# One more pair of k tiles in block products, chunk 8's low part on VectorE, and a planner that knows GpSimd's queue

## The chip, the cores and the metric

The kernel runs on one core of a Trainium2 chip. The metric is device time in microseconds of one execution; lower is better. The five engines of the core that the profile names are TensorE (PE, with PEld for its weight loads), VectorE (DVE), ScalarE (ACT), GpSimd (POOL) and SyncE (SP, which here only requests transfers). Three executions are timed, and one is profiled.

## What is computed

A decoder trunk of two layers over 256 tokens of width 1024, in float32. Layer 0 mixes tokens by a chunked gMLP, layer 1 by block-sparse attention with a shared relative-position bias; each is followed by a gated MLP with a causal convolution of width 3, and each of the four sub-layers ends in a scaled residual and a LayerNorm. What the change touches is the second half of a layer:

```python
D_MODEL, SEQ, DEPTH, FFN_DIM = 1024, 256, 2, 2816
def conv_ffn(x, w_up, conv_w, conv_b, w_down):
    h = x @ w_up                                   # 256x1024 @ 1024x5632
    hp = jnp.pad(h, ((0, 0), (CONV_WIDTH - 1, 0), (0, 0)))
    hc = conv_b
    for j in range(CONV_WIDTH):
        hc = hc + conv_w[j] * hp[:, j:j + S]
    g, val = jnp.split(hc, 2, axis=-1)
    return (jax.nn.gelu(g) * val) @ w_down         # 256x2816 @ 2816x1024
# each sub-layer: x <- LayerNorm(alpha * x + f(x))
# attention adds bias_hb[:, rel_bucket(distance)] to its scores; the table has 32 buckets x 16 heads
```

## The kernel before, in words

**Products in three matmuls.** Every operand is held as two parts: a high part, rounded to the matmul's input type by ScalarE (`act`, L381), and a low part, the difference between the value and its rounding, by VectorE (`tt`, L387). A product is high by high, high by low and low by high, added up in PSUM. The weights of a down projection (2816 x 1024) come as 11 chunks of 1 MB; a chunk holds a pair of k tiles of 128 rows each, all 1024 columns, and goes as one load on SP's queue (`load`, L405) into one of two alternating buffers (`raw_75`, `raw_76`). `prep` then splits it into the tiles `whi` and `wlo`.

**Low parts by an adding transfer.** For the chunks that `ADDED` names, VectorE doesn't subtract: ScalarE writes the high part's negative into the low part's tile, and a transfer that GpSimd requests adds the chunk from memory to it (`lows`, L495). In `f_dn0` and `f_dn1` (the down projections of layers 0 and 1) these are chunks 1, 3 and 8.

**Seven block products.** A pair of k tiles against 256 tokens and 1024 columns is a product of 2 x 2 blocks by 2 x 2 blocks: 8 block products of 128 x 128 by 128 x 512, so 24 matmuls. For the pairs in `SEVEN` it is done by the scheme with seven products and sums of blocks on both sides: 21 matmuls. `weight_sums` makes the sums of weight blocks on VectorE and splits them, with ScalarE, into high and low parts; `token_sums` makes the sums of token blocks on GpSimd, four additions of 128 x 128 each in the tile `lnrow_80` (L634); `token_parts` splits those. `seven` issues the products, and after the last pair `into_rest` adds the common sums to the residual, before the last six k tiles (`TAIL`, chunks 8 to 10) finish the projection. The low parts of these pairs' plain blocks always come by an adding transfer of 0.5 MB (128 x 1024). `KINDS` says where a pair's split sums find room: beside the token parts (`early`, made before the projection starts), in `xt` (the transposed input, free by then), in `rr` (the first token tiles, when they have been used), or in `qk`. The raw rows of such a pair lie in the tile `raw_77`, or, for every other pair (`seven[1::2]`), in a part of the tile `ff`. In `f_dn1` the pairs are 5, 6 and 7.

**The order.** `Plan` records every operation with its engine, an assumed cost, the operations it depends on and a due time, then plays a list schedule for each engine and issues the instructions of an engine in the order of the starts that come out. TensorE's bulk matmuls keep the order in which they are recorded. On the chip an engine runs its instructions in that order and waits where an operand isn't there. Before, GpSimd's adding transfers are planned on an engine of their own, `gq`, beside `pool`, with the token sums; on the chip both are GpSimd's instructions.

**The bias table.** `build_bias` reads the table and a matrix that says which distance belongs to which bucket, rounds them into high and low parts on VectorE (L758, L760) and multiplies them in one matmul (L772), whose result VectorE copies (L774). This happens in the midst of layer 0's down projection. The roundings are recorded there as an operation of TensorE.

**The end of the last projection.** `with_sums` prepares for chunks 8 to 10 a copy of the last 256 columns, with the row sums beside them, in `xt` (ScalarE's operations of 128 x 256 and `xt<-stat` on VectorE), so that the last LayerNorm's mean comes out of the matmuls.

Of the kernel before, what the change touches and what calls it, by code (L numbers as in the profile page):

```python
# [25 lines left out]
NT = S // P  # L26
# [24 lines left out]
SOON = 5000.0  # L51
LEAD = 1700.0
WARM = 9
SEVEN = {"f_dn0": (4, 5, 6), "f_dn1": (5, 6, 7)}


KINDS = {"f_dn0": ('early', 'xt', 'rr'), "f_dn1": ('early', 'rr', 'qk')}


def part7(pairs, kinds):  # L60
# [6 lines left out]


PART7 = {name: part7(pairs, KINDS[name]) for name, pairs in SEVEN.items()}
ADDED = {"f_up0": {13: "act"}, "f_up1": {13: "act"}, "f_dn0": {1: "act", 3: "act", 8: "act"}, "f_dn1": {1: "act", 3: "act", 8: "act"}}  # L70
BESIDE = SEVEN


# [26 lines left out]
class Plan:  # L100
# [1 line left out]

    LATE = {"pe": 200.0, "act": 140.0, "dve": 130.0, "pool": 200.0, "sp": 910.0, "gq": 910.0}

    def __init__(self):
        self.ops, self.line, self.due = [], 0.0, []
# [36 lines left out]
    def emit(self):  # L145
# [24 lines left out]
        for o in ops:  # L170
            left[o] = len(o.deps)
            for d in o.deps:
                succ.setdefault(d, []).append(o)
        engines = ("pe", "act", "dve", "pool", "sp", "gq")
        free = dict.fromkeys(engines, 0.0)
        cand = {e: [] for e in engines}
        bus, table = 0.0, None
        order = []
        bulk = [o for o in ops if o.eng == "pe" and not o.fill]
        nb = 0  # L180
# [7 lines left out]
        while len(order) < len(ops):  # L188
            best = None
            for e in engines:  # L190
                c = cand[e]
                if e == "pe":
                    c = [x for x in c if x[1].fill or (nb < len(bulk) and x[1] is bulk[nb])]
                if not c:
                    continue
                s0 = min(max(free[e], r) for r, _ in c)
                now = [x for x in c if max(free[e], x[0]) <= s0 + 1.0]
                if e == "pe":
                    pick = min(now, key=lambda x: (not x[1].fill, x[1].due))
                else:  # L200
                    pick = min(now, key=lambda x: x[1].due)
                    for x in c:
                        s = max(free[e], x[0])
                        if x[1].due < pick[1].due and s0 < s < s0 + pick[1].ns and \
                                s + x[1].ns <= pick[1].due and x[1].due < s0 + pick[1].ns:
                            pick = x
                s = max(free[e], pick[0])
                if best is None or s < best[0]:
                    best = (s, e, pick)
            s, e, pick = best  # L210
            o = pick[1]
            cand[e].remove(pick)
            if o.eng == "pe" and not o.fill:
                nb += 1
            o.start = s
            if e == "gq":
                bus = max(bus, s + 1100.0) + o.nbytes / 360.0
                free[e] = s + 1200.0
                o.end = max(bus + 1000.0, s + 2000.0 + o.nbytes / 200.0)
            elif e == "sp":  # L220
                bus = max(bus, s + 1100.0) + o.nbytes / 360.0
                free[e] = max(s + 475.0, bus - 1500.0)
                o.end = bus
            else:
                extra = 0.0
                if o.table and o.table != table:
                    extra, table = 1300.0, o.table
                o.end = free[e] = s + o.ns + extra
            order.append(o)
            for x in succ.get(o, ()):  # L230
                left[x] -= 1
                if not left[x]:
                    cand[x.eng].append((ready(x), x))
# [16 lines left out]
        assert not held  # L250

    def lag(self, d, o):
        if d.eng == o.eng:
            return 0.0 if d.eng == "pe" else 910.0 if d.eng in ("sp", "gq") else 130.0
        return self.LATE[d.eng] + (150.0 if o.eng == "pe" else 0.0)


def flat(ap):
    n = 1
    for d in ap.shape[1:]:  # L260
        n *= d
    return n
# [3 lines left out]
def trunk_kernel(ctx: ExitStack, tc: tile.TileContext, a: dict, out: bass.AP):  # L266
# [221 lines left out]
    def lows(i, lv, hv, at, hs, ls, by):  # L488

        name, c = stream[i]  # L490
        if by == "act":
            act(lv, hv.bitcast(F32), AF.Copy, hs, ls, scale=-1.0)
        else:
            dve(70 + 0.52 * flat(lv), lambda: nc.vector.tensor_scalar_mul(lv, hv.bitcast(F32), -1.0), hs, ls)
        plan.op("gq", 3600 + 1.8 * flat(lv), lambda: nc.gpsimd.dma_start(  # L495
            lv, a[name][c][:, at:at + flat(lv)], accum_op=ALU.add, max_dma_last_dim=4 * SUB), (), ls, nbytes=flat(lv) * P * 4)

    def with_sums(key, hi, lo, raw, at):
# [247 lines left out]
    def build_bias(at):  # L746
# [15 lines left out]
        def clear():  # L762
# [5 lines left out]
        plan.op("sp", 4096 / 360, lambda: fill_in(a["rel_bias"], BUCKETS, slice(0, HEADS)), (), [raw], nbytes=4096)  # L768
        plan.op("sp", 65536 / 360, lambda: fill_in(a["onehot"], nb, slice(HEADS, n)), (), [raw], nbytes=65536)
        b = half()  # L770
        plan.op("pe", 645, parts, [raw], [b], True)
        state["table"] = plan.op("pe", 1, lambda: nc.tensor.matmul(  # L772
            b.ap[:HEADS, :DIST], cast[:two, :HEADS], cast[:two, HEADS:], start=True, stop=True), [raw], [b], True)
        dve(400, lambda: nc.vector.tensor_copy(row.ap[:HEADS], b.ap[:HEADS, :DIST]), [b], [row])  # L774
        scr = dram.tile([HEADS, DIST], F32, name="rbscr")
        s = Buf(scr)
        state["bias"] = load(scr, row.ap[:HEADS], [s], [row], nbytes=32768)
# [174 lines left out]
    def project_out(name, nk, at, xold, li, rows_i):  # L952
# [41 lines left out]
        for k, t in sorted(early, key=lambda x: x[1]) if nk == KT else early:  # L994
# [3 lines left out]
            elif k % 2 and t == NT - 1:  # L998
# [7 lines left out]
                if n == len(pairs7) - 1:  # L1006
                    into_rest(xold, extra)
                    by_x = 1.0
            if name == "f_dn0" and (k, t) == (3, NT - 1):
                state["table"].after = groups[-1]  # L1010
            if pairs7 and t == NT - 1:
                for n in range(len(pairs7)):
# [496 lines left out]
```

## Time and profile before

| | |
|---|---|
| time, median of 3 runs | 559.65 us (557.83 to 560.56) |
| profiled execution, its own time | 558.85 us |
| span of the profiled execution | 557.1 us |
| granted TensorE clock | 0.996 |
| PE, busy | 548.8 us (99%), 3024 matmuls |
| DVE, busy | 479.1 us (86%) |
| ACT, busy | 396.5 us (71%) |
| POOL, busy | 51.7 us (9%) |
| moved by the DMA engines | 122.51 MB |

In the profile's views a row of the timeline gives start, length, engine, line of the program, operation, what it writes and reads, and how many instructions it groups; in brackets the idle time of the engine ahead of it, and what ended it. Tiles are named without buffer numbers there: `raw` is any of `raw_75` to `raw_77`, `wlo` any of `wlo_70` to `wlo_74`, `lnrow` the tile of the token sums. The matmuls of a busy TensorE overlap; the step from one start to the next is their price. The last down projection starts at 492.1 us, its first seven block products at 519.3, and its last matmul ends at 550.4.

### The profile page before, as it was taken

The page shows a single profiled execution, that of the slowest core. Times are in us where ns is not written, and L with a number is a line of the kernel's source. Part 1 is how long each engine was busy: PE and PEld are TensorE (multiplying, and loading weights), DVE is VectorE, ACT ScalarE, POOL GpSimd, SP SyncE. Part 2 cuts the span into 40 slices and gives each one's busy share as a digit, 9 for nine tenths or more (in the row PEclk, how much of TensorE's full clock was granted, in tenths as well). Part 3 has the DMA queues.
Part 4 walks back from the last instruction along what each step waited for, and adds up shares of the span by engine and source line. Part 5 has one row for each costly group of instructions (what it writes and reads, how often), then busy time and mean ns, then how long its engine had stood idle before and what let it go on. Part 6 is the DMA issues. An engine that isn't in the chain of part 4 may idle for free.

```text
span 557.1 us, 8253 instructions
## 1 busy us (share of the span) xinstructions
PE 548.8 (99%) x3024; PEld 471.0 (85%) x3024; DVE 479.1 (86%) x860; ACT 396.5 (71%) x669; POOL 51.7 (9%) x60
## 2 busy tenths in 40 slices
PE   9999999999999999999999999999999999999995
PEld 6889888988898887888888888788888888888884
DVE  6699989999989888898957778798969889997687
ACT  6647576688878786845567868577747969897951
POOL 0011110000003521001000000000000000053101
PEclk9999999999999999999999999999999999999998
DMA  8979624645954799893656252725754956799832
GB/s 325 390 284 355 222 99 161 260 184 228 240 213 166 232 283 301 219 356 115 235 218 194 103 191 86 296 77 191 263 188 191 259 203 235 282 268 321 185 100 77
DMA packets 22610, 122.51 MB, mean 220 GB/s; under 512 B 2519, under 2 KB 5801, under 8 KB 10409
## 3 DMA queue, kind: packets, MB, share of 16 engines
q1 hardware_dynamic: 19240, 110.18, 53.4%
q0 software_dynamic: 3040, 11.54, 11.3%
q8 instruction: 24, 0.39, 0.3%
q10 hardware_dynamic: 288, 0.26, 0.1%
q14 instruction: 18, 0.14, 0.1%
HBM read 120.90 MB, written 1.07 MB: 219 GB/s over the span
## 4 chain that ended last, share of the span: by engine, by line
PE 63%; DVE 14%; DMA 12%; ACT 7%; issue 3%; DVEq 0%; SPq 0%; ACTq 0%
PE bank L369 40%; PE twos L369 22%; DVE wlo L387 5%; DMA raw<-in_f_up 5%; DMA raw<-in_f_dn 4%; DVE ff L391 3%; ACT whi L381 3%; DVE ff L387 2%; DMA ff<-in_f_dn 2%; DMA wlo<-in_f_dn 2%; ACT wlo L381 1%; ACT ff L381 1%; DVE x L391 1%; PE twos L375 1%; DVE rr L387 1%
## 5 line engine op out<-in xcount | busy, mean ns | idle before, releaser
L381 ACT ACTIVATE whi<-raw 128x1024 fp32r<-128x1024 f32 (+2 forms) x150 | 175.4, 1203 | 43.4 <-DMA raw<-in_f_up 18.2
L387 DVE TENSOR_TENSOR wlo<-raw,whi 128x1024 fp32r<-128x1024 f32 (+2 forms) x138 | 186.1, 1370 | 18.1 <-ACT whi L381 16.5
L369 PE MATMUL bank<-xt,whi 128*128 128x512 f32 x512 | 121.2, 391 | 0.0
L369 PE MATMUL bank<-whi,rr 128*128 128x512 f32 x354 | 112.5, 391 | 0.0
L369 PEld LDWEIGHTS bank<-xt,whi 128*128 128x128 f32 x512 | 94.7, 188 | 18.7
L369 PEld LDWEIGHTS bank<-whi,rr 128*128 128x128 f32 x354 | 66.5, 188 | 14.0 <-issue 0.3
L369 PE MATMUL twos<-xt,whi 128*128 128x512 f32 x326 | 76.3, 390 | 0.0
L369 PEld LDWEIGHTS twos<-xt,whi 128*128 128x128 f32 x326 | 60.6, 188 | 12.2
L391 DVE SCALAR_TENSOR_TENSOR ff<-ff,convc 128x255 f32<-128x255 f32 (+1 forms) x160 | 69.4, 488 | 0.5
L369 PE MATMUL bank<-wlo,rr 128*128 128x512 f32 x177 | 69.1, 390 | 0.0
L369 PEld LDWEIGHTS bank<-xt,wlo 128*128 128x128 f32 x512 | 64.2, 191 | 2.0 <-issue 0.3
L369 PE MATMUL bank<-xt,wlo 128*128 128x256 f32 x512 | 65.6, 284 | 0.0
L381 ACT ACTIVATE ff<-ff,convc 128x256 f32<-128x256 f32 x80 | 44.5, 593 | 12.2 <-DVE ff L387 12.1
L369 PE MATMUL twos<-whi,xt 128*128 128x512 f32 x128 | 42.1, 396 | 0.0
L369 PE MATMUL twos<-xt,wlo 128*128 128x256 f32 (+1 forms) x323 | 41.2, 284 | 0.0
L369 PEld LDWEIGHTS twos<-xt,wlo 128*128 128x128 f32 x323 | 40.3, 191 | 1.0
L369 PEld LDWEIGHTS bank<-wlo,rr 128*128 128x128 f32 x177 | 33.2, 188 | 6.9 <-DMA wlo<-in_f_dn 0.3
L381 ACT ACTIVATE ff<-bank 128x256 f32<-128x256 f32 (+2 forms) x62 | 23.2, 393 | 17.4 <-PE bank L369 16.4
L381 ACT ACTIVATE ff<-bank,lncol 128x128 f32<-128x128 f32 x48 | 18.9, 458 | 21.0 <-PE bank L375 21.0
L369 PEld LDWEIGHTS twos<-whi,xt 128*128 128x128 f32 x128 | 24.1, 188 | 4.7
L634 POOL TENSOR_TENSOR lnrow<-lnrow 128x128 f32<-128x128 f32 x24 | 22.6, 1130 | 45.5 <-ACT ff L381 37.5
L381 ACT ACTIVATE ff<-twos 128x512 f32<-128x512 f32 (+1 forms) x36 | 18.6, 549 | 9.2 <-PE twos L369 5.7
(158 smaller groups left out, 689.9 us busy)
## 6 DMA issues: line engine op xcount, KB each, us to landing
raw<-in_f_up SPq DMA_DIRECT2D x44, 1024.0 KB, 4.8
raw<-in_f_dn SPq DMA_DIRECT2D x20, 1024.0 KB, 6.3
raw<-in_b_qk SPq DMA_DIRECT2D x8, 1024.0 KB, 4.8
wlo<-in_f_dn POOLq DMA_DIRECT2D x6, 1024.0 KB, 9.1
lnrow<-in_lnrow SPq DMA_DIRECT2D x5, 1024.0 KB, 6.8
raw<-in_a_out SPq DMA_DIRECT2D x4, 1024.0 KB, 7.5
raw<-in_b_v SPq DMA_DIRECT2D x4, 1024.0 KB, 5.0
raw<-in_b_o SPq DMA_DIRECT2D x4, 1024.0 KB, 4.8
```

Of the source, the lines that this page charges most:

```text
L369: nc.tensor.matmul(o, l, x, start=start, stop=stop)
L375: nc.tensor.transpose(o, x, ident.ap)
L381: return plan.op("act", ns, lambda: nc.scalar.activation(o, x, func, **kw), r, w, table=table)
L387: return dve(70 + 1.04 * flat(x), lambda: nc.vector.tensor_tensor(o, x, y, op=op), r, w)
L391: lambda: nc.vector.scalar_tensor_tensor(o, x, s, y, op0=op0, op1=op1), r, w)
L634: plan.op("pool", 1200, lambda: nc.gpsimd.tensor_tensor(o, x, y, op=op), r, w)
```

## The change

It has four parts.

1. `f_dn1` does pairs 4, 5, 6 and 7 by seven block products, not 5, 6 and 7. Pair 4 is now the early one, 5 puts its split sums into `xt`, 6 into `rr`, 7 into `qk`. By the rule on every other pair, 5 and 7 now load into `ff`, and 4 and 6 into `raw_77`. The `xt` copies of `with_sums` wait until pair 5's products have been issued.
2. Chunk 8 leaves `ADDED` in both layers: its low part is a subtraction on VectorE.
3. The planner's engine `gq` goes; GpSimd's adding transfers are planned on `pool`, in one order with its sums, one after another at an assumed rate.
4. The bias table's two roundings are planned as an operation of VectorE, with a tile of their own between them and the matmul, which is put after pair 5's (chunk 2's) matmul group rather than chunk 1's; its copy is given an earlier due time.

```diff
-SEVEN = {"f_dn0": (4, 5, 6), "f_dn1": (5, 6, 7)}
+SEVEN = {"f_dn0": (4, 5, 6), "f_dn1": (4, 5, 6, 7)}
-KINDS = {"f_dn0": ('early', 'xt', 'rr'), "f_dn1": ('early', 'rr', 'qk')}
+KINDS = {"f_dn0": ('early', 'xt', 'rr'), "f_dn1": ('early', 'xt', 'rr', 'qk')}
-ADDED = {"f_up0": {13: "act"}, "f_up1": {13: "act"}, "f_dn0": {1: "act", 3: "act", 8: "act"}, "f_dn1": {1: "act", 3: "act", 8: "act"}}
+ADDED = {"f_up0": {13: "act"}, "f_up1": {13: "act"}, "f_dn0": {1: "act", 3: "act"}, "f_dn1": {1: "act", 3: "act"}}
...
-        engines = ("pe", "act", "dve", "pool", "sp", "gq")
+        engines = ("pe", "act", "dve", "pool", "sp")
...
-            if e == "gq":
+            if e == "pool" and o.nbytes:
                 bus = max(bus, s + 1100.0) + o.nbytes / 360.0
                 free[e] = s + 1200.0
-                o.end = max(bus + 1000.0, s + 2000.0 + o.nbytes / 200.0)
+                added = max(added, s + 1200.0) + o.nbytes / 170.0
+                o.end = added + 2500.0
...
     def lag(self, d, o):
+        if d.eng == "pool" and d.nbytes:
+            return 910.0
         if d.eng == o.eng:
-            return 0.0 if d.eng == "pe" else 910.0 if d.eng in ("sp", "gq") else 130.0
+            return 0.0 if d.eng == "pe" else 910.0 if d.eng == "sp" else 130.0
...
-        plan.op("gq", 3600 + 1.8 * flat(lv), lambda: nc.gpsimd.dma_start(
+        plan.op("pool", 3700 + 3.0 * flat(lv), lambda: nc.gpsimd.dma_start(
...
-        plan.op("pe", 645, parts, [raw], [b], True)
-        state["table"] = plan.op("pe", 1, lambda: nc.tensor.matmul(
-            b.ap[:HEADS, :DIST], cast[:two, :HEADS], cast[:two, HEADS:], start=True, stop=True), [raw], [b], True)
-        dve(400, lambda: nc.vector.tensor_copy(row.ap[:HEADS], b.ap[:HEADS, :DIST]), [b], [row])
+        c = Buf(cast)
+        dve(500, parts, [raw], [c])
+        state["table"] = plan.op("pe", 170, lambda: nc.tensor.matmul(
+            b.ap[:HEADS, :DIST], cast[:two, :HEADS], cast[:two, HEADS:], start=True, stop=True), [c], [b], True)
+        dve(400, lambda: nc.vector.tensor_copy(row.ap[:HEADS], b.ap[:HEADS, :DIST]), [b], [row]).early = 2 * SOON
...
-            if name == "f_dn0" and (k, t) == (3, NT - 1):
+            if name == "f_dn0" and (k, t) == (5, NT - 1):
                 state["table"].after = groups[-1]
```

TensorE in layer 0's down projection, around the bias table's matmul (the only one from `cast`), before:

```order
L369 MATMUL bank_99<-wlo_70,rr 128x512
L369 MATMUL bank_99<-whi_65,rr 128x512
L772 MATMUL twos_96<-cast 16x384
L369 MATMUL bank_100<-whi_66,rr 128x512
L369 MATMUL bank_100<-wlo_71,rr 128x512
```

and after the change (lines of the changed program are three or four higher):

```order
L372 MATMUL bank_99<-wlo_71,rr 128x512
L372 MATMUL bank_99<-whi_66,rr 128x512
L776 MATMUL twos_96<-cast 16x384
L372 MATMUL bank_100<-whi_67,rr 128x512
L372 MATMUL bank_100<-wlo_72,rr 128x512
```

Before, it stands between the groups of chunks 1 (`whi_65`) and 2 (`whi_66`); now between those of chunks 2 and 3 (`whi_67`), 24 matmuls later in TensorE's order.

VectorE in the last down projection, from the sums of the second pair's raw rows to the low parts of the third's, before (pair 6 in `ff`, then pair 7 in `raw_77`):

```order
L387 TENSOR_TENSOR rr<-ff,rr 128x1024
L387 TENSOR_TENSOR ff<-raw_77 128x1024
L387 TENSOR_TENSOR wlo_70<-raw_77,whi_65 128x512
L387 TENSOR_TENSOR raw_77<-raw_77,ff 128x512
L387 TENSOR_TENSOR wlo_70<-ff,whi_65 128x512
L387 TENSOR_TENSOR raw_77<-raw_77 128x512
```

and after the change, where the first raw rows read from `ff` are pair 5's, `raw_77` holds pair 6's, and the second `ff<-ff` of 1024 columns reads pair 7's:

```order
L390 TENSOR_TENSOR xt<-ff,xt 128x1024
L390 TENSOR_TENSOR wlo_74<-lnrow_80,whi_69 128x512
L390 TENSOR_TENSOR ff<-ff 128x512
L390 TENSOR_TENSOR wlo_74<-raw_77,whi_69 128x512
L390 TENSOR_TENSOR ff<-raw_77 128x1024
L390 TENSOR_TENSOR raw_77<-raw_77,ff 128x512
L390 TENSOR_TENSOR ff<-ff 128x1024
L390 TENSOR_TENSOR raw_77<-raw_77 128x512
L390 TENSOR_TENSOR wlo_71<-raw_75,whi_66 128x2048
L390 TENSOR_TENSOR rr<-ff,rr 128x1024
L390 TENSOR_TENSOR rr<-raw_77,rr 128x1024
L390 TENSOR_TENSOR rr<-lnrow_80,rr 128x512
```

Pair 5's last subtraction is `xt<-ff,xt` in the first row; after it its place in `ff` may be loaded again. Pair 7's first difference, `ff<-ff 128x1024`, stands five rows on, ahead of chunk 8's low part (`wlo_71<-raw_75`, 2048 columns, a transfer before) and of the low parts of pair 6 in `rr`.

GpSimd in the last down projection, before:

```order
L495 DMA wlo_73<-in_f_dn 128x1024
L634 TENSOR_TENSOR lnrow_80<-lnrow_80 128x128 x2
L495 DMA wlo_74<-in_f_dn 128x1024
L634 TENSOR_TENSOR lnrow_80<-lnrow_80 128x128 x2
L495 DMA wlo_70<-in_f_dn 128x1024
L495 DMA wlo_71<-in_f_dn 128x2x1024
```

and after the change:

```order
L498 DMA wlo_72<-in_f_dn 128x1024
L637 TENSOR_TENSOR lnrow_80<-lnrow_80 128x128 x6
L498 DMA wlo_73<-in_f_dn 128x1024
L637 TENSOR_TENSOR lnrow_80<-lnrow_80 128x128 x3
L498 DMA wlo_74<-in_f_dn 128x1024
L637 TENSOR_TENSOR lnrow_80<-lnrow_80 128x128
L498 DMA wlo_70<-in_f_dn 128x1024
```

The transfer of 128x2x1024 (1 MB, chunk 8) at the end is gone, one of 128x1024 (0.5 MB) has been added, and the sums of 128x128 between them have gone from four to ten.

SP's last loads of the weights, before:

```order
L405 DMA raw_76<-in_f_dn 128x2048
L405 DMA ff<-in_f_dn 128x2048
L405 DMA raw_77<-in_f_dn 128x2048
L405 DMA raw_75<-in_f_dn 128x2048
L405 DMA raw_76<-in_f_dn 128x2048
```

and after the change:

```order
L408 DMA raw_76<-in_f_dn 128x2048 x2
L408 DMA raw_75<-in_f_dn 128x2048
L408 DMA ff<-in_f_dn 128x2048
L408 DMA raw_77<-in_f_dn 128x2048
L408 DMA ff<-in_f_dn 128x2048
L408 DMA raw_75<-in_f_dn 128x2048
```

Before, the two last chunks' loads follow those of pairs 6 (`ff`) and 7 (`raw_77`); now one of them stands ahead of pair 5's (`ff`), and pair 7's is a second load into `ff`, behind pair 6's (`raw_77`).

More of the change, by code (lines that the diff above doesn't have):

```diff
@@ L100 @@
 class Plan:
-    LATE = {"pe": 200.0, "act": 140.0, "dve": 130.0, "pool": 200.0, "sp": 910.0, "gq": 910.0}
+    LATE = {"pe": 200.0, "act": 140.0, "dve": 130.0, "pool": 200.0, "sp": 910.0}
     def __init__(self):
@@ L173, in emit @@
                 succ.setdefault(d, []).append(o)
-        engines = ("pe", "act", "dve", "pool", "sp", "gq")
+        engines = ("pe", "act", "dve", "pool", "sp")
         free = dict.fromkeys(engines, 0.0)
         cand = {e: [] for e in engines}
-        bus, table = 0.0, None
+        bus, added, table = 0.0, 0.0, None
         order = []
```

## The prediction

> **What bounds the kernel now.** I read the page's first part and TensorE's waits first, since one engine near 100% caps what any edit of another can give.
>
> ```profile
> PE 548.8 (99%) x3024; PEld 471.0 (85%) x3024; DVE 479.1 (86%) x860; ACT 396.5 (71%) x669; POOL 51.7 (9%) x60
> PE twos L1426 <- PEq L1502: 0.8, 1, 0.8
> PE twos L772 <- DVE cast L760: 0.5, 1, 0.5
> PE bank L369 <- DVE whi L412: 0.3, 1, 0.3
> ```
>
> TensorE is busy for 548.8 of 557.1 us and waits for others for 1.6 us in all; so time can be gained only by fewer matmuls or by the one wait of 0.5 us that the edit touches. Time can be lost anywhere, if an engine that feeds it falls behind. Where is one close to that? The chain of waits of the last layer, in order of time (start, length, what):
>
> ```profile
> 499.38 9.03 DMA ff<-in_f_dn
> ...
> 520.92 1.91 ACT wlo L381
> 523.26 8.38 DMA wlo<-in_f_dn
> 531.66 2.85 ACT xt L381 x11
> 534.52 0.49 ACT ff L381
> 535.03 0.69 DVE ff L387
> ```
>
> The last down projection's end isn't set by matmuls: it hangs on a load into `ff`, then on chunk 8's low part (ScalarE's negation, then GpSimd's adding transfer of 8.38 us), then on the sums that open into_rest at 535.03, after which VectorE works nearly without a break to the end. Busy time by stretch, with the columns PE, PEld, DVE, ACT, POOL, granted clock, DMA share and GB/s, cut at that load's landing and at into_rest:
>
> ```profile
> 460.00:508.50 48.50, 48.50 (x261) 42.08 (x260) 45.61 (x72) 41.55 (x61) 11.03 (x13) 1.00 0.83 269
> 508.50:535.00 26.50, 26.50 (x118) 21.91 (x117) 19.97 (x26) 25.27 (x46) 4.83 (x5) 1.00 0.88 232
> ```
>
> In the second stretch VectorE has 6.5 us to spare and ScalarE 1.2. The edit takes place there.
>
> **The change, part by part. TensorE's work.** A pair goes from 24 matmuls to 21. Their price is the step between starts, from the row of 48 in the chain: 10.90/48 = 0.227 us.
>
> ```profile
> 212.18 10.90 PE bank L369 x48
> 211.53 0.17 DVE L760 TENSOR_TENSOR cast<-ff,cast 33x16 fp32r<-33x16 f32 x1
> 211.85 0.34 PE L772 MATMUL twos<-cast 97*16 97x384 f32 x1 [0.46 <-DVE cast L760]
> ```
>
> That is 3 × 0.227 = -0.68 us. The bias table's matmul sat idle for 0.46 us behind VectorE's rounding. It now stands 24 matmuls (5.4 us) later while the rounding keeps its place, so the wait goes: -0.46. The bounds are 0 (the planner shifts the rounding as well) and -0.46; I take all of it. Together -1.14 us: the whole of the possible gain.
>
> **VectorE in the stretch behind the load.** Before, pair 5's products were prepared early and the load into `ff` brought pair 6; now pair 4 is the early one and the load brings pair 5. So three pairs, not two, are prepared between that landing and into_rest, and chunk 8's low part, a subtraction of 2048 columns, comes to VectorE. Its prices are steps between starts in its timeline (start, us, line, operation):
>
> ```profile
> 508.51 1.23 DVE L387 TENSOR_TENSOR ff<-ff 128x1024 f32<-128x1024 f32 x1 [2.79 <-DMA ff<-in_f_dn]
> ...
> 510.72 0.68 DVE L387 TENSOR_TENSOR ff<-ff 128x512 f32<-128x512 f32 x1
> 511.32 0.15 DVE L387 TENSOR_TENSOR xt<-stat,xt 128x2 fp32r<-128x2 f32 x1
> ...
> 515.26 1.21 DVE L387 TENSOR_TENSOR ff<-raw 128x1024 f32<-128x1024 f32 x1
> 516.39 0.68 DVE L387 TENSOR_TENSOR wlo<-raw,whi 128x512 fp32r<-128x512 f32 x1
> ...
> 525.79 2.29 DVE L387 TENSOR_TENSOR wlo<-raw,whi 128x2048 fp32r<-128x2048 f32 x1 [1.11 <-ACT whi L381]
> 528.00 0.68 DVE L387 TENSOR_TENSOR qk<-ff,qk 128x512 fp32r<-128x512 f32 x1
> ```
>
> So 0.60 us for 512 columns, 1.13 for 1024, 2.21 for 2048. From the landing up to pair 6's last low part (the subtraction into `rr` from `lnrow`) VectorE's order has eleven of 512, seven of 1024 and one of 2048: 6.6 + 7.9 + 2.2 = 16.7 us. From there to into_rest come six of 512, one of 1024, two of 2048, one more of 512 and small ones: 10.2 us. In all 26.9 us, where 20 us stood in 26.5.
>
> Before, the same low part was ready when TensorE came:
>
> ```profile
> 523.99 0.69 DVE L387 TENSOR_TENSOR rr<-lnrow,rr 128x512 fp32r<-128x512 f32 x1 [1.71 <-ACT rr L381]
> 525.45 2.20 PE L369 MATMUL twos<-rr 128*128 128x512 f32 x9
> ```
>
> It ended at 524.68 and was read at 525.45. Now TensorE comes at 525.45 - 1.14 = 524.3, and with the landing at 508.5 VectorE is done at 525.2: a stall of 0.9 us even if nothing is waited for.
>
> **The load that has to wait.** Pair 7's rows now go into `ff`, where pair 5's lie, and can be requested only when the subtractions from those are through: five of 512 and three of 1024, 6.4 us behind the landing, so at 514.9. VectorE's order puts pair 7's first difference (`ff<-ff` of 1024 columns) ahead of pair 6's low parts; it is reached four of 512 and one of 1024 later, 3.5 us, at 518.4. What does 1 MB take? From the page, with KB each and the median us to landing:
>
> ```profile
> raw<-in_f_up SPq DMA_DIRECT2D x44, 1024.0 KB, 4.8
> raw<-in_f_dn SPq DMA_DIRECT2D x20, 1024.0 KB, 6.3
> wlo<-in_f_dn POOLq DMA_DIRECT2D x6, 1024.0 KB, 9.1
> ```
>
> The bounds are 4.8 (the loads that mostly run alone) and 9.0 (the load into `ff` above, among others). VectorE then idles for 514.9 + 4.8 - 518.4 = 1.3 us up to 5.5 us. I take the lower end, because chunk 9's load now stands ahead of pair 5's in SP's queue rather than behind pair 6's, and chunk 8's adding transfer is gone: fewer transfers share that time. For the same reason pair 5's rows can land earlier than 508.5, by up to the 2.79 us for which VectorE waited there; I credit 1.0.
>
> **GpSimd.** Its token sums go from 12 to 16 in this projection, and its transfers of 1 MB from three to two, with three of 0.5 MB becoming four. Eight of VectorE's convolution steps, beside five sums and then alone:
>
> ```profile
> 487.72 5.45 POOL L634 TENSOR_TENSOR lnrow<-lnrow 128x128 f32<-128x128 f32 x5 [1.20 <-DVE rr L387]
> 490.36 4.49 DVE L391 SCALAR_TENSOR_TENSOR ff<-ff,convc 128x255 f32<-128x255 f32 x8
> 425.26 3.24 DVE L391 SCALAR_TENSOR_TENSOR ff<-ff,convc 128x255 f32<-128x255 f32 x8
> ```
>
> Five sums cost VectorE 4.49 - 3.24 = 1.25 us, 0.25 each; so four more cost 1.0 us, of which I put half, 0.5, behind the landing (0 to 1.0). The Trainium skill, on its page "SBUF — State Buffer", section "Who interferes with whom", has it that a VectorE operation with two SBUF inputs and a GpSimd operation that reads SBUF exclude each other, the later one being blocked until the other is done. By that four sums would take up to their own 4 × 1.09 = 4.4 us from VectorE; the rows show a slowdown of less than a quarter of that.
>
> **ScalarE.** It loses chunk 8's negation and gains pair 5's roundings.
>
> ```profile
> 519.97 1.04 ACT L381 ACTIVATE rr<-ff 128x1024 fp32r<-128x1024 f32 x1
> 520.92 1.90 ACT L381 ACTIVATE wlo<-whi 128x2048 fp32r<-128x2048 f32 x1
> 522.73 0.70 ACT L381 ACTIVATE xt<-whi 128x256 fp32r<-128x256 f32 x2
> ```
>
> The negation's step is 1.81 us, and a rounding of 1024 is 0.95. Pair 5 brings four of 1024 and two of half that, 4.8 us. About eight of the 256-column copies for the last tile (0.3 each) now follow into_rest's copy instead of preceding it: -2.3. So 25.27 becomes about 26 us of the 26.5. It doesn't set the end by itself, but it leaves no room either: the two engines hand every high and low part to each other, and both are full. Its relief is that into_rest's copy (0.49 at 534.52) no longer stands behind work that waited for chunk 8's transfer; that gives 0.3 to 0.5 us, which I leave uncredited against such hand-over losses.
>
> **Layer 0.** There too VectorE takes chunk 8's low part, 2.3 us as two of 1024. At the end of that projection:
>
> ```profile
> 253.78 1.00 DVE L394 TENSOR_SCALAR x<-x,stat 128x512 f32<-128x512 f32 x2 [0.69 <-POOL stat L794]
> 255.11 1.03 PE L375 MATMUL bank<-ident,x 128*128 128x128 f32 x8
> ```
>
> The slack is 255.11 - 254.78 = 0.33 us, and TensorE comes 0.46 earlier. In the order one subtraction of 1024 moves behind this scaling and another into the 0.69 us in which it waits for GpSimd, so of 2.3 us some 0.5 can remain: 0 to 0.6 us of stall. I take 0, since in this projection VectorE waited for ScalarE, which loses the negation here as well; without that cover it costs the 0.6.
>
> **The sum.** Pair 6's last low part: 508.5 - 1.0 + 16.7 + 1.3 + 0.5 = 526.0 against 524.3, a stall of 1.7; with -1.14, TensorE ends 0.6 us later. into_rest: 508.5 - 1.0 + 26.9 + 1.3 + 0.5 = 536.2 against 535.03, 1.2 us later, and as VectorE is full from there, the end goes with it. The profiled execution took 558.85 us, 0.8 below the median of 559.65; 558.85 + 1.2 = 560.05. I say **560.0 us**: no difference that can be told, since about 0.5% (2.8 us) is what a measurement of this kernel separates from none.
>
> **Rivals.**
> *TensorE alone decides.* Pair 5's rows land about 506, the second load takes 4.8, and the order hides the rest: 558.85 - 1.14 = 557.7 us. For it: VectorE's 2.79 us of waiting for that load. Against it: 26.9 us of work in 26.5.
> *The load into `ff` arrives late: slower.* The place is VectorE's queue, at pair 7's difference; the price is the latency above 4.8. At 6.3 the idle is 2.8, at 9.0 it is 5.5, so the end moves to +2.7 to +5.4 and the time is 561.6 to 564.3; it is slower from a latency of 6.4 on. For it: DMA at 0.88 of its share in this stretch, and 9.03 us for the load before. Against it: the transfers that are gone.
> *The change doesn't do what it says.* The seven products remove matmuls, but the table's rounding shifts with its matmul, GpSimd's order holds adding transfers back behind the new sums, and layer 0 pays 0.6: 560.0 + 0.46 + 0.6 = 561.1.
> *GpSimd's sums shut VectorE out.* If each of the four new sums held a subtraction up for its whole 1.09 us, VectorE would lose 4.4 - 1.0 = 3.4 us more, half of it behind the landing: 561.7. The two rows of eight steps speak against it. This is what the rule of the Trainium skill named above would do here.
>
> **How the numbers follow.** My forecast has 0.42, TensorE alone 0.26, the late load 0.23, the third 0.07 and GpSimd's sums 0.02. Slower by over 0.5% is most of the late load and a little of the rest, 0.23; faster by over 0.5% needs more than the 1.14 us that can be gained, 0.05; the same 0.72. The range reaches from TensorE alone, 557.7, to a latency of 8.0 (idle 4.5, +4.4), 563.2; the likeliest case's own is 558.5 to 561.5.
>
> **What would show it.** Right: no wait at the table's matmul; 21 matmuls per pair for four pairs; VectorE idle at pair 7's `ff<-ff` for 1 to 2 us, released by the DMA into `ff`; a TensorE wait of 1 to 2 us at the nine matmuls from `rr`; into_rest near 536. Wrong: VectorE's stretch free of waits with into_rest at or before 535, or a TensorE wait elsewhere (at 255, or in the convolution's up projection, whose order has also shifted).

## The result and the profile after

The changed kernel takes 564.32 us (median of 9 runs, 563.04 to 568.25) against 559.65 us before (median of 9, 557.52 to 562.79): 1.0101 times as long, with a 95% interval from 1.0073 to 1.0130. The forecast was no difference that can be told, at 560.0 us, with a range up to 563.2; the kernel is slower, and outside the range. The profiled execution took 565.05 us, its span is 563.4 us, 6.3 us more than before.

TensorE's waits after the change:

```profile
PE bank L372 <- DMA wlo<-in_f_dn: 3.5, 2, 3.2
PE bank L372 <- DVE whi L415: 1.1, 1, 1.1
PE twos L1430 <- PEq L1506: 0.8, 1, 0.8
```

The wait at the bias table's matmul is gone, as forecast. A new one of 3.2 us stands at a low part `wlo` that comes by an adding transfer; the other in that row, 0.4 us at 206.27, is at chunk 1's low part. The 1.1 us at `whi` are at the start of the program and cost nothing: at 6 us the two kernels are level. The timeline of TensorE shows where, and what follows it (start, length, operation):

```profile
217.06 0.34 PE L776 MATMUL twos<-cast 97*16 97x384 f32 x1
217.24 0.40 PE L372 MATMUL bank<-whi,rr 128*128 128x512 f32 x1
220.79 0.51 PE L372 MATMUL bank<-wlo,rr 128*128 128x512 f32 x1 [3.16 <-DMA wlo<-in_f_dn]
...
222.36 0.63 PE L372 MATMUL bank<-wlo,rr 128*128 128x512 f32 x1
222.79 1.05 PE L372 MATMUL bank<-whi,rr 128*128 128x512 f32 x2
223.64 0.63 PE L372 MATMUL bank<-wlo,rr 128*128 128x512 f32 x1
...
259.92 1.11 PE L378 MATMUL bank<-ident,x 128*128 128x128 f32 x8
```

It isn't in the last projection, of which the prediction spoke, but in layer 0's, at chunk 3, right behind the bias table. And it costs more than its length: from 222.2 to 225.6 the matmuls step by 0.43 us (222.36 to 222.79) instead of 0.227. The transposes at the end of this projection start at 259.92, and before the change at 255.11: 4.8 us of the 6.3 have been lost by then. At TensorE's last matmul it is 5.4 us (it ends at 555.8, before at 550.4), and what follows that takes 7.6 us instead of 6.7; these smaller losses haven't been followed. Busy time and granted clock (the figure behind POOL's) in four stretches around the wait:

```profile
212.00:217.50 5.50, 5.50 (x26) 4.26 (x24) 5.27 (x10) 3.57 (x5) 2.16 (x5) 1.00 1.04 298
217.50:220.75 3.25, 0.14 (x1) 0.00 (x0) 2.04 (x3) 1.63 (x2) 0.00 (x0) 1.00 1.04 311
220.75:228.00 7.25, 7.21 (x24) 5.75 (x25) 7.11 (x10) 6.77 (x8) 1.78 (x2) 0.76 1.05 236
228.00:236.00 8.00, 8.00 (x37) 6.62 (x36) 6.67 (x6) 4.51 (x7) 0.00 (x0) 1.00 0.70 233
```

The clock granted behind the wait is 0.76 for 7.25 us: 24 matmuls where 32 would fit, a loss of about 1.8 us. GpSimd's timeline shows why the low part is late:

```profile
191.90 1.24 POOL L498 DMA_DIRECT2D wlo<-in_f_dn  x1 [52.28 <-ACT wlo L384]
195.77 2.63 POOL L637 TENSOR_TENSOR lnrow<-lnrow 128x128 f32<-128x128 f32 x3 [2.64 <-DVE rr L390]
206.48 1.22 POOL L498 DMA_DIRECT2D wlo<-in_f_dn  x1 [8.08 <-ACT ff L384]
207.26 2.50 POOL L637 TENSOR_TENSOR lnrow<-lnrow 128x128 f32<-128x128 f32 x3
```

and ScalarE's the operation on which the second of these transfers depends, the negation of chunk 3's high part:

```profile
198.86 1.91 ACT L384 ACTIVATE wlo<-whi 128x2048 fp32r<-128x2048 f32 x1
```

Chunk 1's transfer is requested at 191.90. Chunk 3's could follow at 200.8, when the negation is done, and follows at 206.48; the releaser that the row names, ScalarE's `ff`, isn't among its operands. Chunk 1's transfer took 14.3 us, so it landed at 206.2: chunk 3's request stood until then. The same place before the change:

```profile
191.13 1.24 POOL L495 DMA_DIRECT2D wlo<-in_f_dn  x1 [2.90 <-ACT wlo L381]
191.92 4.62 POOL L634 TENSOR_TENSOR lnrow<-lnrow 128x128 f32<-128x128 f32 x4
201.36 1.22 POOL L495 DMA_DIRECT2D wlo<-in_f_dn  x1 [4.83 <-ACT wlo L381]
```

There chunk 1's took 8.9 us (landed at 200.1), and chunk 3's was requested at 201.36. What the DMA queues moved from 191 to 196 us, after the change and before it (q0 carries GpSimd's requests, q1 SP's; packets, MB, share):

```profile
q1 hardware_dynamic: 244, 1.84, 96.2%
raw<-in_f_dn SPq DMA_DIRECT2D x1, 1024.0 KB, 10.6
wlo<-in_f_dn POOLq DMA_DIRECT2D x1, 1024.0 KB, 14.3
```

```profile
q0 software_dynamic: 119, 0.49, 62.3%
raw<-in_f_dn SPq DMA_DIRECT2D x2, 1024.0 KB, 8.6
wlo<-in_f_dn POOLq DMA_DIRECT2D x1, 1024.0 KB, 8.9
```

After the change two loads (chunk 3's at 189.0 and chunk 2's at 189.4) are under way when the adding transfer is requested, and in these 5 us not one packet of it moves; its first comes at 196.4, 4.5 us behind the request. Before, no load was under way, and the first packet came 2.0 us behind the request; the two loads of 195 came behind it. So the start is 2.5 us later than usual, and the rest of the delay comes beside the next load, of 195.8: there the adding transfer moves some 0.1 MB a microsecond where it moves 0.2 alone.

Why are two loads requested together? Chunk 3's load stands ahead of chunk 2's in both kernels. What has changed in SP's order is that chunk 0's load comes ahead of chunk 1's, not behind it. Chunk 2 goes into chunk 0's buffer, which is free when VectorE has subtracted chunk 0's low part. Before and after the change:

```profile
192.60 2.42 DVE L387 TENSOR_TENSOR wlo<-raw,whi 128x2048 fp32r<-128x2048 f32 x1 [1.42 <-ACT whi L381]
```

```profile
184.75 2.28 DVE L390 TENSOR_TENSOR wlo<-raw,whi 128x2048 fp32r<-128x2048 f32 x1
```

Before, that held chunk 2's load until 195.05, 9.3 us behind chunk 3's (185.78) and behind the adding transfer. Now nothing holds it but its place in SP's order, and it goes 0.4 us behind chunk 3's, ahead of the adding transfer.

In the last projection the profile is near the prediction's sum, not its parts. VectorE between the landing in `ff` and into_rest:

```profile
511.95 2.02 DVE L390 TENSOR_TENSOR ff<-ff 128x1024 f32<-128x1024 f32 x2 [2.09 <-DMA ff<-in_f_dn]
...
517.79 0.94 DVE L390 TENSOR_TENSOR rr<-ff,rr 128x512 fp32r<-128x512 f32 x1
...
523.99 1.22 DVE L390 TENSOR_TENSOR ff<-ff 128x1024 f32<-128x1024 f32 x1
...
530.20 0.68 DVE L390 TENSOR_TENSOR rr<-lnrow,rr 128x512 fp32r<-128x512 f32 x1
...
541.73 0.68 DVE L390 TENSOR_TENSOR ff<-twos,ff 128x512 f32<-128x512 f32 x1
```

### The profile page after: what moved, and what is told of

Its sections match the earlier page's. It is cut to its first block, busy times and chain, and to the rows that moved or that the text cites. A ratio compares the mean times of both kernels' runs of the same rounds, so it can differ in the third digit from the quotient of the medians.

```text
span 563.4 us, 8274 instructions
## 1 busy us (share of the span) xinstructions
PE 550.2 (98%) x3021; PEld 470.4 (84%) x3021; DVE 488.5 (87%) x869; ACT 396.5 (70%) x673; POOL 49.6 (9%) x63
## 4 chain that ended last, share of the span: by engine, by line
PE 83%; DMA 6%; ACT 5%; DVE 4%; issue 2%; DVEq 0%; ACTq 0%
PE bank L372 48%; PE twos L372 32%; DMA wlo<-in_f_dn 3%; ACT whi L384 2%; DMA ff<-in_f_dn 2%; PE twos L378 1%; PE bank L378 1%; DVE x L394 1%; DMA raw<-in_f_dn 1%; ACT wlo L384 1%; ACT ff L384 1%; DVE ff L390 1%; DMA ff<-in_head 1%; ACT xt L384 0%; DVE wlo L390 0%
## 5 line engine op out<-in xcount | busy, mean ns | idle before, releaser
L390 DVE TENSOR_TENSOR wlo<-raw,whi 128x1024 fp32r<-128x1024 f32 (+2 forms) x140 | 188.0, 1363 | 16.8 <-ACT whi L384 16.1
L372 PE MATMUL bank<-whi,rr 128*128 128x512 f32 x340 | 110.1, 395 | 0.0
L372 PE MATMUL twos<-xt,whi 128*128 128x512 f32 x332 | 78.1, 390 | 0.0
L372 PEld LDWEIGHTS bank<-whi,rr 128*128 128x128 f32 x340 | 64.7, 190 | 14.5 <-DVE rr L390 0.4
L372 PE MATMUL bank<-wlo,rr 128*128 128x512 f32 x170 | 67.3, 396 | 3.5 <-DMA wlo<-in_f_dn 3.5
L390 DVE TENSOR_TENSOR ff<-twos,ff 128x512 f32<-128x512 f32 (+2 forms) x34 | 21.8, 653 | 5.3 <-ACT ff L384 3.5
```

What stands on the lines that cost most here:

```text
L372: nc.tensor.matmul(o, l, x, start=start, stop=stop)
L390: return dve(70 + 1.04 * flat(x), lambda: nc.vector.tensor_tensor(o, x, y, op=op), r, w)
```

## The experiments

Theory A: the loss is made in layer 0 by the order of transfers that parts 3 and 4 bring (GpSimd's queue, the bias table). Theory B: it is the work that parts 1 and 2 add to VectorE and ScalarE. The first four runs set the one against the other. All ratios are to the kernel before, with 95% intervals.

### The added work without the new planner: the kernel before with parts 1 and 2

```diff
-SEVEN = {"f_dn0": (4, 5, 6), "f_dn1": (5, 6, 7)}
+SEVEN = {"f_dn0": (4, 5, 6), "f_dn1": (4, 5, 6, 7)}
-KINDS = {..., "f_dn1": ('early', 'rr', 'qk')}
+KINDS = {..., "f_dn1": ('early', 'xt', 'rr', 'qk')}
-ADDED = {..., "f_dn0": {1: "act", 3: "act", 8: "act"}, "f_dn1": {1: "act", 3: "act", 8: "act"}}
+ADDED = {..., "f_dn0": {1: "act", 3: "act"}, "f_dn1": {1: "act", 3: "act"}}
```

> The kernel before with parts 1 and 2 of the change alone (four pairs, chunk 8's low part on VectorE); the planner and the bias table stay as before. Theory A (the loss is the order of layer 0's transfers, made by parts 3 and 4: 3.2 us of waiting for chunk 3's adding transfer, about 1.7 us of lower clock behind it; the rest, 1.2 us, is VectorE's in the last projection): layer 0 keeps its order, chunk 3's adding transfer lands near 211 as before, no wait there, 559 to 561.5 us. Theory B (the added work of VectorE and ScalarE costs the time, wherever it then shows): 563 to 565 us.

Measured: 559.19 us, ratio 1.0025 (1.0003 to 1.0048). Chunk 3's transfer lands at 209.8, and TensorE doesn't wait for it. Theory B falls: all the work that the change adds costs a quarter of a percent here.

### The new planner without the added work: the kernel before with parts 3 and 4

```diff
-        engines = ("pe", "act", "dve", "pool", "sp", "gq")
+        engines = ("pe", "act", "dve", "pool", "sp")
...
-        plan.op("gq", 3600 + 1.8 * flat(lv), lambda: nc.gpsimd.dma_start(
+        plan.op("pool", 3700 + 3.0 * flat(lv), lambda: nc.gpsimd.dma_start(
...
-        plan.op("pe", 645, parts, [raw], [b], True)
+        dve(500, parts, [raw], [c])
...
-            if name == "f_dn0" and (k, t) == (3, NT - 1):
+            if name == "f_dn0" and (k, t) == (5, NT - 1):
```

> The kernel before with parts 3 and 4 alone (GpSimd's queue and the bias table as planned now); three pairs and chunk 8 by an adding transfer, as before. Theory A: GpSimd's order in layer 0 is that of the change (three sums, chunk 3's transfer, three sums), TensorE waits about 3 us for chunk 3's low part near 217 with the granted clock near 0.8 for some 8 us behind it, 562.5 to 565 us. Theory B: no such wait, 559 to 560 us, by 0.5 less than before for the table's wait.

Measured: 565.05 us, ratio 1.0126 (1.0097 to 1.0155). GpSimd's queue in layer 0:

```profile
192.58 1.24 POOL L498 DMA_DIRECT2D wlo<-in_f_dn  x1 [52.30 <-ACT wlo L384]
196.46 2.63 POOL L637 TENSOR_TENSOR lnrow<-lnrow 128x128 f32<-128x128 f32 x3 [2.63 <-DVE rr L390]
206.34 1.22 POOL L498 DMA_DIRECT2D wlo<-in_f_dn  x1 [7.25 <-ACT wlo L384]
```

It is the changed kernel's, its times within 0.7 us, with a wait of 3.4 us at chunk 3 and a granted clock of 0.76 for the 7 us behind it. As theory A has it. (TensorE also waits 1.7 us in layer 1's up projection, which the changed kernel doesn't.)

### Chunk 3's low part on VectorE, in the changed kernel

```diff
-"f_dn0": {1: "act", 3: "act"}
+"f_dn0": {1: "act"}
```

> The changed kernel, with chunk 3 of layer 0's down projection no longer among those with an adding transfer: VectorE subtracts (2.2 us more for it), ScalarE's negation (1.8 us) and 1 MB of adding transfer fall away. Theory A: the wait of 3.2 us near 217 and the lower clock behind it go, unless another transfer takes their place; 559 to 561 us. Theory B: VectorE has still more to do, 564 to 567 us.

Measured: 559.96 us, ratio 1.0025 (1.0004 to 1.0045). The wait at 217 is gone; VectorE's 2.2 us more show as a wait of 1.3 us for pair 6's low part at 235. Here only one load of 1 MB ran when chunk 1's transfer was requested, and it took 8.2 us.

### Chunk 3's adding transfer in halves, in the changed kernel

```diff
+        if (name, c) == ("f_dn0", 3):
+            for j, l in enumerate(ls):
+                ...
+                plan.op("pool", 3700 + 3.0 * SUB, half_of, (), [l], nbytes=SUB * P * 4)
+            return
```

> The changed kernel, with chunk 3's adding transfer in layer 0 requested as two of 0.5 MB instead of one of 1 MB. Its request stood at 206.5, 5.7 us after its operands were ready and 0.3 us after chunk 1's transfer of 1 MB had landed. If GpSimd's queue takes no second transfer of 1 MB while one is under way, but takes 0.5 MB (as it did at 208.9), the first half is requested near 201 and the second near 206.5: the wait near 217 shrinks to 0 to 2 us, 560 to 563 us. If any second transfer is held until chunk 1's lands, or something else holds the queue, both are requested at 206 to 207 and the wait stays near 3 us, 563.5 to 565 us.

The time was a miss: 578.49 us, ratio 1.0368 (1.0333 to 1.0404). The question for which it was made it answers. GpSimd in layer 0:

```profile
191.50 1.24 POOL L504 DMA_DIRECT2D wlo<-in_f_dn  x1 [52.28 <-ACT wlo L384]
195.38 2.87 POOL L643 TENSOR_TENSOR lnrow<-lnrow 128x128 f32<-128x128 f32 x4 [2.64 <-DVE rr L390]
200.68 0.91 POOL L501 DMA_DIRECT2D wlo<-in_f_dn  x1 [2.42 <-ACT wlo L384]
205.30 0.85 POOL L501 DMA_DIRECT2D wlo<-in_f_dn  x1 [3.71 <-issue]
```

Chunk 1's transfer took 13.5 us and landed at 205.0. The first half of chunk 3's went out at 200.68 beside it, the second only at 205.30, held by nothing that the profile shows ("issue"). So 1.5 MB of adding transfers were under way together, and 2 MB were not. The wait at 217 is gone. But the planner, given other operations, ordered the last layer otherwise, and the same pair of events came up there: chunk 1's transfer of that projection took 13.9 us, and chunk 3's was requested 0.3 us after it had landed. In all TensorE waited 12.7 us for adding transfers, in three places of the last projection and at one other of layer 0's.

### One part at a time, each in the kernel before

The planner's queue alone (part 3):

```diff
-            if e == "gq":
+            if e == "pool" and o.nbytes:
...
-        plan.op("gq", 3600 + 1.8 * flat(lv), lambda: nc.gpsimd.dma_start(
+        plan.op("pool", 3700 + 3.0 * flat(lv), lambda: nc.gpsimd.dma_start(
```

> The kernel before with part 3 alone (GpSimd's adding transfers planned in one queue with its sums). Theory A in its narrower form: what decides is the order of requests in layer 0. Where chunk 1's adding transfer is requested right behind two loads it moves nothing until they are through and lands 13 to 14 us later, and GpSimd then holds chunk 3's request until it has landed; where loads follow it, it lands within 9 us. If part 3 makes the harmful order, chunk 1's transfer takes 13 us or more, TensorE waits about 3 us at chunk 3, 562.5 to 565 us; if not, it takes about 9 us and the time is 558.5 to 560 us. Rival: the loss comes from seven sums ahead of chunk 3's transfer on GpSimd itself, then it shows here whatever the landing of chunk 1's.

Measured: 564.56 us, ratio 1.0119 (1.0085 to 1.0152), a miss for the expectation. Chunk 1's transfer took 8.5 us, and there is no wait at chunk 3, so neither theory A's place nor the rival (the sums ahead of chunk 3's transfer) is seen. Its losses lie elsewhere:

```profile
PE twos L775 <- DVE cast L763: 1.7, 1, 1.7
PE bank L372 <- DMA wlo<-in_f_dn: 1.2, 1, 1.2
```

The bias table's wait has grown to 1.7 us, and another adding transfer is waited for in the last projection. That these make up its whole loss hasn't been followed further.

The bias table alone (part 4):

```diff
-        plan.op("pe", 645, parts, [raw], [b], True)
+        dve(500, parts, [raw], [c])
...
-            if name == "f_dn0" and (k, t) == (3, NT - 1):
+            if name == "f_dn0" and (k, t) == (5, NT - 1):
```

> The kernel before with part 4 alone (the bias table's roundings as an operation of VectorE, the matmul 24 matmuls later). By the prediction's step: the table's wait of 0.46 us goes, 558.2 to 559.5 us. By theory A, if part 4 is what moves the loads ahead of chunk 1's adding transfer: that transfer takes 13 us or more, a wait of about 3 us at chunk 3 and a lower clock behind it, 562.5 to 565 us.

Measured: 568.21 us, ratio 1.0187 (1.0158 to 1.0216), slower than either expectation. The table's wait is gone, and chunk 1's transfer in layer 0 takes 8.3 us; but TensorE waits 7.0 us for adding transfers in three places, one in layer 0 at a pair's plain blocks and two in layer 1. There the order differs again: chunk 1's transfer, with one load requested 0.3 us behind it and another 3.2 us behind it, takes 14.4 us, and chunk 3's goes out 0.3 us after it has landed and takes 13.9. So neither part alone makes the harmful order in layer 0, and both together do: in the programs, chunk 1's load comes ahead of chunk 0's in each run of this list with one part alone and in that with parts 1 and 2, and its transfer in layer 0 takes 8.3 to 9.0 us there; with parts 3 and 4 together chunk 0's comes first, and it takes 13.5. The bias table alone makes one in layer 1; the queue alone loses its time at other waits.

The four pairs alone (part 1):

```diff
-SEVEN = {"f_dn0": (4, 5, 6), "f_dn1": (5, 6, 7)}
+SEVEN = {"f_dn0": (4, 5, 6), "f_dn1": (4, 5, 6, 7)}
-KINDS = {..., "f_dn1": ('early', 'rr', 'qk')}
+KINDS = {..., "f_dn1": ('early', 'xt', 'rr', 'qk')}
```

> The kernel before with part 1 alone: pairs 4 to 7 in seven products, chunk 8's adding transfer kept. Theory A: layer 0 is untouched; what differs is the last projection, where VectorE has 4 us more and chunk 8's transfer stays in GpSimd's queue beside four others. By the prediction's sum VectorE is the later one there by 1.2 us, less the 2.2 us that chunk 8 adds: 558 to 560 us. If pair 7's wait for its place in ff, or the adding transfers, set the end: 560.5 to 562 us.

Measured: 568.65 us, ratio 1.0185 (1.0159 to 1.0211), worse than either expectation. Layer 0 is nearly as before (a wait of 0.5 us for an adding transfer at 243). In the last projection the longest wait is 4.4 us, at pair 7's plain blocks. The two last adding transfers, chunk 8's and pair 7's, are requested within a microsecond of each other (with KB and the us to landing):

```profile
wlo<-in_f_dn POOLq DMA_DIRECT2D x1, 1024.0 KB, 8.3
wlo<-in_f_dn POOLq DMA_DIRECT2D x1, 512.0 KB, 12.6
```

Chunk 8's 1 MB goes first, and pair 7's 0.5 MB, which TensorE needs earlier, lands behind it at 537.9. Without part 2 part 1 costs 10 us; with it (559.19 us above) next to nothing. The prediction had taken chunk 8's step to VectorE for a cost of 2.2 us; it is what makes room for the fourth pair.

Chunk 8 alone (part 2):

```diff
-ADDED = {..., "f_dn0": {1: "act", 3: "act", 8: "act"}, "f_dn1": {1: "act", 3: "act", 8: "act"}}
+ADDED = {..., "f_dn0": {1: "act", 3: "act"}, "f_dn1": {1: "act", 3: "act"}}
```

> The kernel before with part 2 alone: chunk 8's low part on VectorE, three pairs. Theory A: layer 0's transfers stay in their order, one adding transfer of 1 MB less in each layer; VectorE has 2.3 us more in each, where it had 6.5 us to spare in the last projection: 558 to 560 us. If VectorE's place at the end of layer 0 (slack 0.33 us) decides, 560 to 561 us.

Measured: 558.06 us, ratio 0.9991 (0.9980 to 1.0003): no difference.

### Chunk 1's transfer taken away, in the changed kernel

```diff
-"f_dn0": {1: "act", 3: "act"}
+"f_dn0": {3: "act"}
```

> The changed kernel with chunk 1 of layer 0's down projection taken from those with an adding transfer. Theory A: chunk 3's request is no longer held, it stands near 201, right behind ScalarE's negation, and lands by 211 to 213; no wait at chunk 3; 559 to 561 us. If chunk 3's request still stands near 206, something else in GpSimd's queue holds it and the wait stays, 563 to 565 us.

Measured: 559.29 us, ratio 1.0013 (0.9999 to 1.0028). Chunk 3's transfer, now the first of this projection, is requested when its negation is done:

```profile
200.82 1.24 POOL L498 DMA_DIRECT2D wlo<-in_f_dn  x1 [61.52 <-ACT wlo L384]
205.43 2.04 POOL L637 TENSOR_TENSOR lnrow<-lnrow 128x128 f32<-128x128 f32 x1 [3.37 <-PE bank L372]
```

and the whole loss is gone. It was chunk 1's transfer that held it. (Chunk 3's own took 12.0 us here, which its earlier request covers.)

### The load ahead of it cut short, in the changed kernel

```diff
+        short = [(raw.ap[:, :P], src[:, :P])] if (name, c) == ("f_dn0", 2) else None
-        loads[i] = load(raw.ap[:, :CH], src, [(raw, range(CH // 256))], halves=i in HALVES)
+        loads[i] = load(raw.ap[:, :CH], src, [(raw, range(CH // 256))], halves=i in HALVES, real=short)
```

> The changed kernel, instruction for instruction in the same order, but the load of layer 0's chunk 2 (requested at 189.4, 2.5 us ahead of chunk 1's adding transfer, one of two loads under way then) brings only 128 of the 2048 columns; the rest of the buffer keeps old data, so that part of the down projection is left out in value. Theory A (the adding transfer is starved by the loads that were requested ahead of it): with one load ahead of it, as in the kernels where it took 8 to 9 us, it lands near 200 to 201 instead of 206.2, chunk 3's request follows near 201, the wait of 3.2 us is gone or under 0.5 us, 558.5 to 560.5 us. Rival (it is slow for its own sake, or through GpSimd's three sums at 195.8, which stay): it still takes 13 us or more, the wait stays, 563 to 565 us.

Measured: 558.88 us, ratio 1.0001 (0.9990 to 1.0012). The order of every engine is the changed kernel's; one load is shorter by 15/16. GpSimd's queue:

```profile
191.38 1.24 POOL L499 DMA_DIRECT2D wlo<-in_f_dn  x1 [52.28 <-ACT wlo L384]
195.25 2.64 POOL L638 TENSOR_TENSOR lnrow<-lnrow 128x128 f32<-128x128 f32 x3 [2.64 <-DVE rr L390]
200.60 1.22 POOL L499 DMA_DIRECT2D wlo<-in_f_dn  x1 [2.71 <-ACT wlo L384]
```

Chunk 1's transfer takes 8.8 us and lands at 200.1, chunk 3's is requested at 200.60 rather than 206.48, and the only wait that is left on TensorE is the 0.8 us of the start. So the chain of causes is shown link by link: the load of chunk 2 beside that of chunk 3, chunk 1's transfer behind them, chunk 3's request behind that, TensorE's wait, and the lowered clock. This run leaves a part of the work out, so its time is a bound for a better order, not a kernel: the change without its harmful place in layer 0 is as fast as the kernel before, and no faster.

## Why the prediction was wrong

*TensorE's work and the table's wait.* Right. The table's matmul waits for nothing any more, and three matmuls are fewer.

*The step that failed* is the search for the places where time could be lost. "The edit takes place there", it said of the last projection. The edit of the planner takes place in every stage: it moves GpSimd's requests and SP's loads in layer 0, and there a term of +5 us was left at 0 to 0.6. The prediction's section on layer 0 costed VectorE alone, where there was indeed no stall. Its third rival named the right engine (GpSimd's order holding adding transfers back) and gave it 0.07 and 561.1 us, with 0.6 us for the whole of layer 0; but it put the hold on the new sums, and what held chunk 3's transfer was chunk 1's. The question that was not asked is when chunk 3's low part is needed and when it lands. In the trace of before it is read at 217.7 and landed at 210.7 (201.36 and its 9.3 us): 7 us of slack. In the changed kernel it landed at 220.75, 10 us later, half of it through chunk 1's transfer and half through its own, which took 14.3 us beside three loads and another adding transfer. Of the prediction's signs, two of being right were seen (no wait at the table's matmul, 21 matmuls for each of four pairs); in the last projection VectorE doesn't wait at pair 7's difference, nor TensorE at the nine matmuls from `rr`. What was seen instead is its sign of being wrong, a TensorE wait elsewhere.

*The last projection.* The terms were right in sum, and partly in kind. From the landing to pair 6's last low part I had 16.7 + 1.3 + 0.5 = 18.5 us; the profile shows 511.95 to 530.88, 18.9. But the 1.3 us of waiting for pair 7's rows in `ff` don't exist: the last packet of the load asked for at 517.9 came at 522.5, and VectorE came to it only at 523.99. Five of its steps beside GpSimd's work are some 0.27 us longer than usual (0.87 instead of 0.60 between starts at 517.79), 1.3 us where 0.5 was put in, and at 516.40 it has waited 0.36 us for ScalarE. The stretch from 511.95 to there took 12.0 us and not 9.9. The two errors cancel, which is luck. In the run with the short load, where nothing else disturbs, into_rest begins at 535.4, against 536.2 forecast and 535.03 before, because the rows landed 2.9 us earlier than before and not 1.0. In that run the last projection costs TensorE no wait at all: the stall of 1.7 us forecast at the matmuls from `rr` isn't there, since pair 6's last low part is ready at 524.54 and read at 524.60. The slower rival (a late load into `ff`) doesn't occur either. Yet the run is no faster than the kernel before: into_rest is 0.35 us later, and the end, as the prediction had it, doesn't follow TensorE alone (its last matmul ends 1.0 us earlier than before, the span 0.6).

*Chunk 8.* I had it as a cost to VectorE that its transfer's disappearance didn't quite pay. Alone it is neutral; with four pairs it is worth about 9 us (ratios to the kernel before of 1.0185 without it and 1.0025 with it).

*GpSimd's exclusion of VectorE.* By the Trainium skill's rule ("SBUF — State Buffer", "Who interferes with whom") each sum could block a subtraction for its whole length. Beside an idle VectorE a sum takes 0.44 us (two in 0.88 at 509.94), and the steps beside the sums are 0.27 us longer: more than half of that length, not the whole, and the time of this change isn't decided by it. The prediction misread one of its two rows. Of the five sums one took 3.04 us, beside VectorE's subtraction of 2048 columns at 488.16, and the other four 0.64 each, beside the convolution steps; so 1.09 us is the mean of two kinds, 1.25 us over four sums are 0.31 each and not 0.25, and there it was a sum of GpSimd that was held up most.

## What to carry to other kernels

A change to a planner's rules is a change of every queue that it plans: compare the order and the times of requests in all stages, the DMA queues above all, and not only where the work has changed. For each transfer that a saturated engine waits for, write down when it is needed, when it landed, and how many transfers stand ahead of it; slack of 7 us was gone here when a second load of 1 MB came to run ahead of two adding transfers that follow each other in GpSimd's queue, and what had changed was the order of two loads before it. And a transfer taken off a queue can be worth more than the engine time which replaces it.

## What the runs showed of the hardware

*An adding transfer that meets running loads starts late.* In the profiles of these kernels chunk 1's adding transfer of 1 MB took 8.1 to 9.2 us where at most one load of 1 MB had more than 0.6 us to go at its request and the next came 3.9 us or more behind it. It took 13.5 to 14.4 us in five cases: in three of them two loads were under way, in two a load was requested 0.2 and 0.3 us behind it and another some 3 us behind it. The first packet came 1.9 to 2.3 us behind the request in the quick cases and 4.2 to 5.0 us in the slow ones, about when the load's data were through: from 191.9 to 196.4 the changed kernel moved 1.55 MB, all of it for SP. The two groups aren't a rule for every transfer: chunk 3's, with one load under way and the next 4.0 us behind it, took 12.0 us in the run without chunk 1's. Where the adding transfer comes first, the loads behind it are the ones that slow down (10.3 us for one, before the change). The Trainium skill, "DMA: Bandwidth & Descriptors", section "Queues, rings and completion order", has each DMA engine take turns between its queues, packet by packet. By that GpSimd's transfer, if it had packets ready after its usual 2 us, would have had a share from 193.9 on, and the trace shows none before 196.4; whether they were ready isn't shown. Later, from 200 to 206.5, both queues move (0.41 MB for GpSimd, 1.05 for SP).

*Two adding transfers of 1 MB weren't under way together* in any of these profiles, though operands were ready up to 5.7 us before; 1 MB with 0.5 MB was common, and it was never more than that. The request stands in GpSimd's queue, and everything behind it waits too. The profile names an unrelated releaser there.

*A wait of TensorE can lower the clock behind it, and its length alone doesn't decide.* Behind 3.2 us (the changed kernel) it was 0.76 over 7 us, behind 2.6 and 2.9 us (the bias table alone) 0.72 and 0.73 over 6, and behind 2.3 us (chunk 3 in halves, 503 to 505.4) 0.83 over 10. But in that same run it stayed at 1.00 behind waits of 2.9 us (518.2 to 521.2) and of 3.6 us, the second longest there:

```profile
231.04 0.50 PE L372 MATMUL bank<-wlo,rr 128*128 128x512 f32 x1 [3.61 <-DMA wlo<-in_f_dn]
228.00:235.00 7.00, 3.96 (x17) 3.30 (x18) 7.00 (x7) 5.07 (x7) 0.00 (x0) 1.00 0.88 255
```

Behind single waits of 1.3 and 1.5 us it stayed at 1.00 too, though three short ones within 2.5 us, 1.4 us in sum (the four pairs alone, 525 to 533), brought 0.79. In the changed kernel the clock is still 1.00 from 220.80, when the wait is over, to 222.10, then 0.50 to 225.55 and 1.00 again from 225.65, which added 1.8 us to the wait. Each lowered stretch in the midst of these profiles lasts 3.41 us, and two in one profile start a whole number of such lengths apart (505.81 and 546.76 with chunk 3 in halves). If one cuts each profile into such periods, an estimate from these traces alone, TensorE stood idle for 2.0 us or more of the period before the stretch in seven of eight cases and 1.5 in the eighth, and for 1.9 us at most in every period that none follows: the wait of 3.6 us lay across a border. The Trainium skill, "TensorE: Matmul & The Clock Gate", section "What's actually happening", has the clock fall to half after an idle window of about 3.4 us; the step of 0.43 us instead of 0.227 agrees with the half, and waits of 2.3 to 2.9 us were already enough here.
